# FFN up with adding DMAs: a weight sum and three low parts per pair of columns formed on GpSimd's queue

## The chip, the cores and the metric

The kernel runs on one NeuronCore of a Trainium2 chip. The core has a matrix engine (TensorE, "PE" in the profile, with its weight loads as "PEld"), a vector engine (VectorE, DVE), a scalar engine (ScalarE, ACT), a general one (GpSimd, POOL), a synchronising engine (SyncE, SP) that here only issues transfers, and 16 DMA engines that all queues share. The metric is the time of one execution on the device in microseconds (us), as the median of repeated runs. A profile of one execution shows each instruction on each engine.

## What is computed

A trunk of two decoder layers on 512 tokens of width 1024 in float32. Each layer has a mixer (dilated attention beside a state-space block in the first, a gated linear recurrence in the second) and a SwiGLU feed-forward block, each between two RMS norms. The change touches only the feed-forward block's first half:

```python
def swiglu(x, w_gate, w_up, w_down):
    return (jax.nn.silu(x @ w_gate) * (x @ w_up)) @ w_down
...
        hn = rms_norm(x, norm_ffn_pre[layer])
        ff = swiglu(hn, ffn_w_gate[layer], ffn_w_up[layer], ffn_w_down[layer])
        x = x + rms_norm(ff, norm_ffn_post[layer])
```

The hidden width is 2816, which is 22 blocks of 128 columns for the gate and 22 for the up matrix.

## The kernel before

Products are made to nearly float32 precision from a shorter format ("fp32r"): each operand is split into a high part (a rounded copy) and a low part (the operand less its high part), and three matmuls (high x high, high x low, low x high) stand for one. Activations lie transposed, features on the 128 partitions and tokens along a row of 512.

**FFN up** (`ffn_up`, line 598). The first two pairs of columns (a gate block and an up block make a pair n) are done plainly. The other 20, n = 2 to 21, go through the loop at line 694 with a fast scheme for 2x2 block matrices (Strassen's idea in Winograd's form). The blocks are a gate column's two halves over the input width, a11 and a12, an up column's two halves, a21 and a22, and the two halves of the tokens. Seven products take the place of eight. For this the weights are combined first, in `pair_weights` (line 636): s1 = a21 + a22 (line 644), s2 = s1 - a11, a21 is overwritten by a11 - a21, and s4 = a12 - s2. Each of these tiles holds 128 partitions x 512 values, as 4 blocks of 128 x 128 weights.

**Chunks.** `Raw` (line 205) takes tiles and loads them by DMAs on SP's queue, 256 KB each (line 216), 128 partitions x 4 rows of 512 bytes. `Chunk` (line 221) forms, for each raw tile, the high part on ACT (line 240) and the low part on DVE (line 241), and gives the raw tile back. A pair has four chunks. "a" is the gate column (tiles a11, a12), "c" the sums (s1, s4), "d" the up column (its first tile overwritten by a11 - a21, its second a22 as loaded), "b" has s2 alone. That makes 7 high parts on ACT and 4 + 7 operations on DVE per pair. The names in the trace carry layer, pair and chunk: `wlo_f010a` is the low part of chunk a of pair 10 in layer 0. `wraw_f` is a loaded tile, `wraw_s_f` a tile of s1 or s4, `wraw_t_f` one of s2.

**Products and what follows.** `product` (line 690) runs 4 blocks x 3 matmuls of 256 tokens; seven of them make a pair. ACT moves three of the products out of PSUM (lines 707 to 711), DVE combines the rest (lines 720 to 726), ACT takes the SiLU and DVE multiplies (lines 614 and 616).

**Order.** All engines run at once, each in the order of its own list of instructions, and wait on one another by semaphores. A scheduler makes these lists when the program is built, from a model of the times, except where the code pins an order. Tiles for raw weights and parts come from one list of places (`place`, line 194); a load waits on SP until the tile that it overwrites was last read, so prefetch runs as far ahead as there are free places. GpSimd is all but unused in this stage: it has the power of the row norm (line 383), which the first evacuations need, and in the stages before and after it some additions to the residual (line 502).

Of the kernel before, what the change touches and what calls it, by code (L numbers as in the profile page):

```python
# [11 lines left out]
F32 = mybir.dt.float32  # L12
F32R = mybir.dt.float32r
I32 = mybir.dt.int32
AF = mybir.ActivationFunctionType
ALU = mybir.AluOpType
# [3 lines left out]
P = 128  # L20
S = 512
D = 1024
NF = D // P
# [71 lines left out]
def hybrid_trunk(  # L95
# [8 lines left out]
    nc = tc.nc  # L104
    dve, act, pool = nc.vector, nc.scalar, nc.gpsimd
# [88 lines left out]
    def place(nm, dtype, base=None):  # L194
        p = next(p for p in places if base is None or p[0] is base)
        places.remove(p)
        return p[0].tile([P, S], dtype, tag=p[1], name=nm), p

    def give(ps):
        places.extend(p for p in ps if p not in retired)  # L200

    def shaped(t, n):
        return t.rearrange("p (k n) -> p k n", n=n)

    class Raw:


        def __init__(self, nk, n, nm, src=None, base=None):
            self.n, self.step = n, S // n
            self.parts, self.places = [], []  # L210
            for i in range(0, nk, self.step):
                t, p = place(f"wraw_{nm}_{i}", F32, base)
                self.parts.append(shaped(t, n))
                self.places.append(p)
                if src is not None:
                    nc.sync.dma_start(self.parts[-1], src[:, i:i + self.step])
# [4 lines left out]
    class Chunk:  # L221


        def __init__(self, raw, nm, alloc=None, view=None, base=None, eng=None):
            n, self.step = raw.n, raw.step
            eng = eng or dve
            self.places, self.parts = [], []
            for i, src in enumerate(raw.parts):
                pair = []
                for q in ("hi", "lo"):  # L230
                    if alloc is not None:
                        t = alloc(f"w{q}_{nm}_{i}")
                    else:
                        t, p = place(f"w{q}_{nm}_{i}", F32R, base)
                        self.places.append(p)
                    pair.append(shaped(t, n))
                self.parts.append(pair)
                hi, lo = pair
                if view is None:
                    act.activation(hi, src, AF.Copy)  # L240
                    eng.tensor_tensor(lo, src, hi.bitcast(F32), op=ALU.subtract)  # L241
                else:
                    for j in range(self.step):
                        r = src[:, j].rearrange("p (q g c) -> p q g c", g=8, c=CH)
                        act.activation(view(hi[:, j]), r, AF.Copy)
                        dve.tensor_tensor(view(lo[:, j]), r, view(hi[:, j]).bitcast(F32), op=ALU.subtract)
                give(raw.places[i:i + 1])
# [347 lines left out]
    def ffn_cols(layer):  # L595
        return [(w[layer], n * P) for n in range(NH) for w in (ffn_w_gate, ffn_w_up)]

    def ffn_up(layer, xh, xl, first, nsum, nm, hp):
# [4 lines left out]
        cols2 = ffn_cols(layer)  # L603
        hidden = []
        env = {}
        HK = NF // 2
# [28 lines left out]

        def pair_weights(n, alloc=None, base=None):

            r0, r1 = [Raw(NF, P, f"{nm}{n}{i}", cols2[2 * n + i][0][:, n * P:(n + 1) * P].rearrange(
                "(k p) n -> p k n", p=P), base=base) for i in range(2)]
            (a11, a12), (a21, a22) = r0.parts, r1.parts  # L640
            rs = Raw(NF, P, f"s_{nm}{n}", base=base)
            rt = Raw(HK, P, f"t_{nm}{n}")
            (s1, s4), (s2,) = rs.parts, rt.parts
            dve.tensor_tensor(s1, a21, a22, op=ALU.add)  # L644
            dve.tensor_tensor(s2, s1, a11, op=ALU.subtract)  # L645
            dve.tensor_tensor(a21, a11, a21, op=ALU.subtract)
            dve.tensor_tensor(s4, a12, s2, op=ALU.subtract)
            return [Chunk(t, f"{nm}{n}{q}", alloc=alloc) for t, q in ((r0, "a"), (rs, "c"), (r1, "d"), (rt, "b"))]

        own = iter([*range(11, NH), 3, 4, 5, 6])  # L650
        for q in range(NFIRST // 2 + 3):
            retired.add((hp, f"hh{q}"))
        wa, wc, wd, wb = pair_weights(
            NFIRST // 2, lambda name: hp.tile([P, S], F32R, tag=f"hh{next(own)}", name=name), sb)

# [3 lines left out]
        for k in range(HK):  # L659
            a = hp.tile([P, S], F32, tag=f"hh{7 + k % 2}", name=f"xa_{nm}{k}")  # L660
            b = hp.tile([P, S], F32, tag=f"hh{9 + k % 2}", name=f"xb_{nm}{k}")
            act.activation(a, xT[k], AF.Copy, scale=col("g1", layer * NF + k))
            act.activation(b, xT[k + HK], AF.Copy, scale=col("g1", layer * NF + k + HK))
            raw = Raw(4, HT, f"tr_{nm}{k}")
# [29 lines left out]
        for n in range(NFIRST // 2, NH):  # L694
            if n > NFIRST // 2:
                for q in range(n + 3):
                    retired.add((hp, f"hh{q}"))
                places[:] = [p for p in places if p not in retired]
                wa, wc, wd, wb = pair_weights(n)
# [971 lines left out]
```

## Time and profile before

| | |
|---|---|
| three runs | 1168.99, 1170.04, 1175.23 us; median 1170.04 us |
| the profiled execution | 1169.77 us in all, span from first to last instruction 1167.7 us |
| granted PE clock | 0.99 of full speed |
| DMA traffic | 113.45 MB, mean 97 GB/s; SP's queue 32.2% of the 16 engines' time |
| FFN up, layer 0 and layer 1 | about 295 to 490 us and 845 to 1040 us of the span |
| FFN weights on SP's queue | 88 loads of gate tiles, 88 of up tiles, 256 KB each, landing a median 3.1 and 3.3 us after issue |

The profile gives, for each engine, its busy time in any stretch, the instructions by source line and tile, who waited for whom, and the chain of work that ended last, followed back from the last instruction. Busy time alone does not say what a change is worth: an engine that nobody waits for can get faster without effect. A matmul's row is longer than its share of time, because matmuls overlap; the count of matmuls in a stretch says how fast PE goes on. For DMA instructions the row gives the time of issuing; when the data lands is told apart.

### The profile page before, as it was taken

What the parts mean: (1) busy time and instruction counts of PE and PEld (TensorE: products, weight loads), DVE (VectorE), ACT (ScalarE), POOL (GpSimd) and SP (SyncE); (2) the same over time, 40 slices, a digit from 0 to 9 for tenths busy, and PEclk for the clock granted to TensorE, in tenths of its full rate; (3) what the DMA queues carried; (4) which work ended last, traced back from release to release, by engine and by line L of the source; (5) the groups of instructions that cost most, each with busy time, mean ns of one, the idle gap of its engine ahead of it and who ended that gap; (6) DMA issues with size and microseconds to landing.
All of it is one profiled execution on the core that took longest, in us unless ns stands there. A gap on an engine that the chain in (4) does not pass through costs nothing.

```text
span 1167.7 us, 20255 instructions
## 1 busy us (share of the span) xinstructions
PE 1131.7 (97%) x7550; PEld 1013.2 (87%) x7550; DVE 876.8 (75%) x1841; ACT 626.6 (54%) x1290; POOL 60.6 (5%) x100
## 2 busy tenths in 40 slices
PE   6999899999999999999999999999999999999997
PEld 6877666889999999988889887889999999988886
DVE  7989675478999899882345887956999899984224
ACT  7556576357655555652244479744855455582221
POOL 1000010003000000000004000004000000000001
PEclk9999989999999999999999999999999999999999
DMA  8534410522333332423330323430253333334221
GB/s 211 144 117 134 108 45 1 172 64 63 93 109 100 101 99 83 125 92 96 121 100 1 106 86 98 126 109 1 77 146 95 101 109 91 90 119 126 91 63 72
DMA packets 165561, 113.45 MB, mean 97 GB/s; under 512 B 26852, under 2 KB 142296, under 8 KB 165464
## 3 DMA queue, kind: packets, MB, share of 16 engines
q1 hardware_dynamic: 162168, 109.95, 32.2%
q10 hardware_dynamic: 3040, 2.17, 0.7%
q8 instruction: 59, 0.97, 0.3%
q14 instruction: 38, 0.31, 0.1%
q0 software_dynamic: 256, 0.06, 0.0%
HBM read 103.75 MB, written 4.19 MB: 92 GB/s over the span
## 4 chain that ended last, share of the span: by engine, by line
PE 82%; DVE 5%; ACT 5%; DMA 4%; issue 2%; POOL 0%; ACTq 0%; DVEq 0%; POOLq 0%; SPq 0%
PE fo L170 10%; PE op_fd L170 10%; PE op_mo L170 6%; PE f00b L170 5%; PE f02b L170 5%; PE f01b L170 4%; PE f11b L170 4%; PE f10b L170 4%; PE f12b L170 4%; PE qkv L170 4%; PE gg L170 3%; PE f03b L170 2%; PE f13b L170 2%; PE mo1b L170 2%; PE mo0b L170 2%; PE xbb L170 2%
## 5 line engine op out<-in xcount | busy, mean ns | idle before, releaser
L241 DVE TENSOR_TENSOR wlo_fo<-wraw_fo,whi_fo 128x512 fp32r<-128x512 f32 x44 | 30.3, 691 | 63.8 <-PE fo L170 58.7
L170 PE MATMUL op_fd<-hi_f,whi_fd 128*128 128x512 f32 (+1 forms) x200 | 73.7, 369 | 0.0
L170 PE MATMUL op_fd<-lo_f,whi_fd 128*128 128x512 f32 (+1 forms) x200 | 73.4, 367 | 0.0
L170 PE MATMUL op_fd<-hi_f,wlo_fd 128*128 128x512 f32 (+1 forms) x200 | 73.0, 367 | 0.0
L170 PE MATMUL fo<-wlo_fo,hi_f 128*128 128x512 f32 x176 | 69.4, 394 | 0.0
L170 PE MATMUL fo<-whi_fo,lo_f 128*128 128x512 f32 x176 | 69.1, 394 | 0.0
L170 PE MATMUL fo<-whi_fo,hi_f 128*128 128x512 f32 x176 | 68.9, 396 | 0.0
L240 ACT ACTIVATE whi_fo<-wraw_fo 128x512 fp32r<-128x512 f32 x44 | 27.6, 631 | 70.6 <-DMA wraw_fo<-in_ffn_w_down_dram 43.4
L241 DVE TENSOR_TENSOR wlo_fd<-wraw_fd,whi_fd 128x512 fp32r<-128x512 f32 x44 | 30.1, 690 | 46.4 <-ACT whi_fd L240 42.5
L240 ACT ACTIVATE whi_fd<-wraw_fd 128x512 fp32r<-128x512 f32 x44 | 27.4, 629 | 54.7 <-DMA wraw_fd<-in_ffn_w_down_dram 33.8
L170 PEld LDWEIGHTS op_fd<-lo_f,whi_fd 128*128 128x128 f32 x200 | 37.7, 189 | 6.8
L170 PEld LDWEIGHTS op_fd<-hi_f,wlo_fd 128*128 128x128 f32 x200 | 37.7, 189 | 6.7
L170 PEld LDWEIGHTS op_fd<-hi_f,whi_fd 128*128 128x128 f32 x200 | 37.7, 189 | 6.6
L170 PE MATMUL qkv<-whi_qkv,xh_m 128*128 128x512 f32 x96 | 40.5, 427 | 0.0
L170 PEld LDWEIGHTS fo<-whi_fo,lo_f 128*128 128x128 f32 x176 | 33.1, 188 | 7.8
L170 PEld LDWEIGHTS fo<-whi_fo,hi_f 128*128 128x128 f32 x176 | 33.1, 188 | 7.7
L170 PEld LDWEIGHTS fo<-wlo_fo,hi_f 128*128 128x128 f32 x176 | 33.1, 188 | 7.5
L170 PE MATMUL qkv<-wlo_qkv,xh_m 128*128 128x512 f32 x96 | 38.3, 399 | 0.0
L170 PE MATMUL qkv<-whi_qkv,xl_m 128*128 128x512 f32 x96 | 38.0, 396 | 0.0
L644 DVE TENSOR_TENSOR wraw_s_f<-wraw_f,wraw_f 128x512 f32<-128x512 f32 x40 | 27.4, 684 | 11.4 <-DMA wraw_f<-in_ffn_w_up_dram 10.7
L241 DVE TENSOR_TENSOR wlo_mo<-wraw_mo,whi_mo 128x512 fp32r<-128x512 f32 x32 | 21.4, 686 | 14.5 <-ACT whi_mo L240 14.2
L645 DVE TENSOR_TENSOR wraw_t_f<-wraw_s_f,wraw_f 128x512 f32<-128x512 f32 x40 | 27.3, 682 | 6.0 <-DMA wraw_f<-in_ffn_w_gate_dram 6.0
(1974 smaller groups left out, 4297.8 us busy)
## 6 DMA issues: line engine op xcount, KB each, us to landing
wraw_f<-in_ffn_w_gate_dram SPq DMA_DIRECT2D x88, 256.0 KB, 3.1
wraw_f<-in_ffn_w_up_dram SPq DMA_DIRECT2D x88, 256.0 KB, 3.3
wraw_fd<-in_ffn_w_down_dram SPq DMA_DIRECT2D x44, 256.0 KB, 2.8
wraw_fo<-in_ffn_w_down_dram SPq DMA_DIRECT2D x44, 256.0 KB, 2.9
wraw_qkv<-in_ev_w_in_dram SPq DMA_DIRECT2D x24, 256.0 KB, 3.5
wraw_mo<-in_ev_w_out_dram SPq DMA_DIRECT2D x16, 256.0 KB, 4.3
wraw_xb<-in_od_w_in_dram SPq DMA_DIRECT2D x16, 256.0 KB, 2.8
wraw_gg<-in_od_w_in_dram SPq DMA_DIRECT2D x16, 256.0 KB, 2.8
```

The lines of the kernel that those rows point to most:

```text
L170: self.pin(nc.tensor.matmul(o, lhsT=lhsT, rhs=rhs, start=start, stop=stop, **kw))
L240: act.activation(hi, src, AF.Copy)
L241: eng.tensor_tensor(lo, src, hi.bitcast(F32), op=ALU.subtract)
L644: dve.tensor_tensor(s1, a21, a22, op=ALU.add)
L645: dve.tensor_tensor(s2, s1, a11, op=ALU.subtract)
```

## The change

Two things in the FFN up's pairs move from DVE to DMAs that add while they write, issued on GpSimd's queue.

- **The sum s1.** The tile of s1 is loaded with a21 by one more plain DMA on SP, and a22 is then added onto it from DRAM by an adding DMA on GpSimd. The addition on DVE goes.
- **Three low parts per pair**, those of tiles that are plain weights: both tiles of chunk a and the second of chunk d. ACT writes the negated high part to the low tile (a copy with scale -1 into the same short format), and an adding DMA on GpSimd adds the weights onto it from DRAM. The subtraction on DVE goes. The other four low parts (s1, s4, s2 and a11 - a21 are not in DRAM) stay on DVE.

Per pair that is four DVE operations fewer, three ACT operations more, one plain load more and four adding DMAs, of 256 KB each; 40 pairs in the two layers.

```diff
-        def __init__(self, raw, nm, alloc=None, view=None, base=None, eng=None):
+        def __init__(self, raw, nm, alloc=None, view=None, base=None, eng=None, dram=None):
...
                     act.activation(hi, src, AF.Copy)
-                    eng.tensor_tensor(lo, src, hi.bitcast(F32), op=ALU.subtract)
+                    if dram is not None and dram[i] is not None:
+                        act.activation(lo, src, AF.Copy, scale=-1.0)
+                        pool.dma_start(lo, dram[i], accum_op=ALU.add)
+                    else:
+                        eng.tensor_tensor(lo, src, hi.bitcast(F32), op=ALU.subtract)
...
         def pair_weights(n, alloc=None, base=None):
 
-            r0, r1 = [Raw(NF, P, f"{nm}{n}{i}", cols2[2 * n + i][0][:, n * P:(n + 1) * P].rearrange(
-                "(k p) n -> p k n", p=P), base=base) for i in range(2)]
+            src = [cols2[2 * n + i][0][:, n * P:(n + 1) * P].rearrange("(k p) n -> p k n", p=P) for i in range(2)]
+            rs = Raw(NF, P, f"s_{nm}{n}", base=base)
+            (s1, s4) = rs.parts
+            nc.sync.dma_start(s1, src[1][:, 0:HK])
+            pool.dma_start(s1, src[1][:, HK:NF], accum_op=ALU.add)
+            r0, r1 = [Raw(NF, P, f"{nm}{n}{i}", src[i], base=base) for i in range(2)]
             (a11, a12), (a21, a22) = r0.parts, r1.parts
-            rs = Raw(NF, P, f"s_{nm}{n}", base=base)
             rt = Raw(HK, P, f"t_{nm}{n}")
-            (s1, s4), (s2,) = rs.parts, rt.parts
-            dve.tensor_tensor(s1, a21, a22, op=ALU.add)
+            (s2,) = rt.parts
             dve.tensor_tensor(s2, s1, a11, op=ALU.subtract)
             dve.tensor_tensor(a21, a11, a21, op=ALU.subtract)
             dve.tensor_tensor(s4, a12, s2, op=ALU.subtract)
-            return [Chunk(t, f"{nm}{n}{q}", alloc=alloc) for t, q in ((r0, "a"), (rs, "c"), (r1, "d"), (rt, "b"))]
+            same = {"a": [src[0][:, 0:HK], src[0][:, HK:NF]], "d": [None, src[1][:, HK:NF]]}
+            return [Chunk(t, f"{nm}{n}{q}", alloc=alloc, dram=same.get(q))
+                    for t, q in ((r0, "a"), (rs, "c"), (r1, "d"), (rt, "b"))]
```

How the lists move is seen best on GpSimd. Around the start of layer 0's FFN up its list read, before (the residual's last additions, the row norm's power, and then already the end of the FFN):

```order
L502 TENSOR_TENSOR xT_4_151<-xT_4_151,o_mo04_2932 128x256
L502 TENSOR_TENSOR xT_5_152<-xT_5_152,o_mo05_2934 128x256
L502 TENSOR_TENSOR xT_6_153<-xT_6_153,o_mo06_2936 128x256
L502 TENSOR_TENSOR xT_7_154<-xT_7_154,o_mo07_2938 128x256
L383 TENSOR_TENSOR rsy_f0_3486<-rst_f0_3485,neghalf_133 128x4
L383 TENSOR_TENSOR rsy_fd00_7567<-rst_fd00_7566,neghalf_133 128x2
```

and now, at the same place:

```order
L506 TENSOR_TENSOR xT_7_154<-xT_7_154,o_mo07_2938 128x256
L243 DMA wlo_f02a_0_3514<-in_ffn_w_gate_dram 128x4x128
L646 DMA wraw_s_f03_0_3735<-in_ffn_w_up_dram 128x4x128
L243 DMA wlo_f02a_1_3519<-in_ffn_w_gate_dram 128x4x128
L243 DMA wlo_f02d_1_3536<-in_ffn_w_up_dram 128x4x128
L387 TENSOR_TENSOR rsy_f0_3486<-rst_f0_3485,neghalf_133 128x4
L646 DMA wraw_s_f04_0_3887<-in_ffn_w_up_dram 128x4x128
```

Four adding DMAs now stand ahead of the row norm's power. In the middle of the stage, where GpSimd's list had nothing, it now has, for pairs 8 to 12 (L243 a low part, L646 a sum):

```order
L243 DMA wlo_f08a_1_4517<-in_ffn_w_gate_dram 128x4x128
L646 DMA wraw_s_f09_0_4647<-in_ffn_w_up_dram 128x4x128
L243 DMA wlo_f08d_1_4534<-in_ffn_w_up_dram 128x4x128
L243 DMA wlo_f09a_0_4664<-in_ffn_w_gate_dram 128x4x128
L646 DMA wraw_s_f010_0_4799<-in_ffn_w_up_dram 128x4x128
L243 DMA wlo_f09a_1_4669<-in_ffn_w_gate_dram 128x4x128
L646 DMA wraw_s_f011_0_4951<-in_ffn_w_up_dram 128x4x128
L243 DMA wlo_f09d_1_4686<-in_ffn_w_up_dram 128x4x128
L243 DMA wlo_f010a_0_4816<-in_ffn_w_gate_dram 128x4x128
L243 DMA wlo_f010a_1_4821<-in_ffn_w_gate_dram 128x4x128
L646 DMA wraw_s_f012_0_5103<-in_ffn_w_up_dram 128x4x128
```

Sums of pairs 10 and 11 come ahead of low parts of pair 9, in one queue. On DVE, between the evacuations of pairs 6 and 7, the list read before (`gt`, `ut`, `pu`: tiles of the evacuation):

```order
L241 TENSOR_TENSOR wlo_f09d_1_4655<-wraw_f091_4_4625,whi_f09d_1_4654 128x512
L645 TENSOR_TENSOR wraw_t_f09_0_4629<-wraw_s_f09_0_4627,wraw_f090_0_4619 128x512
L646 TENSOR_TENSOR wraw_f091_0_4623<-wraw_f090_0_4619,wraw_f091_0_4623 128x512
L721 TENSOR_TENSOR gt_f07_4459<-f00b7_4366,bcs_f0_3495 128x256
L241 TENSOR_TENSOR wlo_f09c_0_4643<-wraw_s_f09_0_4627,whi_f09c_0_4642 128x512
L722 TENSOR_TENSOR pu_f07_4370<-pu_f07_4370,f01b7_4367 128x256
L724 TENSOR_TENSOR pu_f07_4370<-pu_f07_4370,f02b7_4368 128x256
L644 TENSOR_TENSOR wraw_s_f010_0_4775<-wraw_f0101_0_4771,wraw_f0101_4_4773 128x512
L241 TENSOR_TENSOR wlo_f010a_0_4783<-wraw_f0100_0_4767,whi_f010a_0_4782 128x512
L616 TENSOR_TENSOR hh_f06_4321<-ut_f06_4312,gt_f06_4311 128x512
```

and now, at the evacuation of pair 7:

```order
L729 TENSOR_TENSOR gt_f07_4483<-f00b7_4390,bcs_f0_3495 128x256
L245 TENSOR_TENSOR wlo_f09c_0_4674<-wraw_s_f09_0_4647,whi_f09c_0_4673 128x512
L730 TENSOR_TENSOR pu_f07_4394<-pu_f07_4394,f01b7_4391 128x256
L651 TENSOR_TENSOR wraw_t_f010_0_4811<-wraw_s_f010_0_4799,wraw_f0100_0_4803 128x512
L731 TENSOR_TENSOR ut_f07_4484<-pu_f07_4394,pv_f07_4395 128x256
L245 TENSOR_TENSOR wlo_f09c_1_4678<-wraw_s_f09_4_4648,whi_f09c_1_4677 128x512
L732 TENSOR_TENSOR pu_f07_4394<-pu_f07_4394,f02b7_4392 128x256
L653 TENSOR_TENSOR wraw_s_f010_4_4800<-wraw_f0100_4_4805,wraw_t_f010_0_4811 128x512
L245 TENSOR_TENSOR wlo_f09d_0_4682<-wraw_f091_0_4655,whi_f09d_0_4681 128x512
```

The sum of pair 10 (L644) and the low parts `wlo_f010a` and `wlo_f09d_1` are gone from DVE; the sums' consumers (L651, L653) stand at about the same distance ahead of the products.

## The prediction

> **What bounds the kernel now.** I read the page's busy times first, then the stretches of the FFN-up stages, then who waits for whom in them.
>
> ```profile
> PE 1131.7 (97%) x7550; PEld 1013.2 (87%) x7550; DVE 876.8 (75%) x1841; ACT 626.6 (54%) x1290; POOL 60.6 (5%) x100
> ```
>
> PE is busy nearly all the time. The change touches only the two FFN-up stages. The view by stretches gives, for the steady middle of each and for each as a whole, the length, then the busy time of PE, PEld, DVE, ACT and POOL, the granted clock, the DMA share and the rate in GB/s.
>
> ```profile
> 350.00:460.00 110.00, 110.00 (x927) 110.00 (x926) 102.27 (x204) 57.29 (x117) 0.00 (x0) 1.00 0.34 97
> 850.00:950.00 100.00, 99.39 (x833) 98.99 (x833) 94.73 (x189) 53.39 (x108) 0.00 (x0) 1.00 0.40 114
> 297.00:486.00 189.00, 186.16 (x1557) 185.20 (x1555) 178.66 (x353) 101.47 (x207) 0.00 (x0) 1.00 0.34 99
> 843.00:1041.00 198.00, 195.90 (x1621) 193.41 (x1620) 187.02 (x371) 110.37 (x226) 0.00 (x0) 1.00 0.38 110
> ```
>
> A pair needs 84 matmuls (7 products x 4 blocks x 3). From 350 to 460 us there are 927, so 927/84 = 11.04 pairs in 110 us: **9.97 us of PE per pair**. PE has no gap there. DVE comes close, 102.27/11.04 = 9.26 us per pair, ACT uses 5.19 us, POOL nothing, and the DMA engines a third. So the stage is PE-bound, with DVE a hair behind. All that PE idles in the two stages is 189 - 186.16 = 2.8 us and 198 - 195.90 = 2.1 us. By PEld it is 3.8 and 4.6 us. **The most that a lighter DVE can bring is thus 5 to 8 us**, and not all of that is DVE's. The gaps lie at the stage's start and end, and the chain that ended last shows what they are (start, length, what):
>
> ```profile
> 291.86 0.89 PE bc_f L170 x8
> ...
> 307.82 3.64 DMA wraw_f<-in_ffn_w_gate_dram
> ...
> 312.70 0.28 ACT pu_f L709
> ...
> 467.35 2.80 DMA wraw_f<-in_ffn_w_up_dram
> ```
>
> Both large ones begin with a load of a raw weight tile, and only then pass ACT and DVE.
>
> **What is taken off DVE and put on ACT.** Rows of the raw weight tiles between 350 and 400 us (durations in ns, minimum, median, maximum):
>
> ```profile
> L644 DVE TENSOR_TENSOR wraw_s_f<-wraw_f,wraw_f x5: 679/681/682, 351.3 to 391.6; 128x512 f32<-128x512 f32 x5
> L240 ACT ACTIVATE whi_f010a<-wraw_f x2: 632/633/634, 353.0 to 357.4; 128x512 fp32r<-128x512 f32 x2
> L241 DVE TENSOR_TENSOR wlo_f010a<-wraw_f,whi_f010a x2: 678/678/679, 359.2 to 363.6; 128x512 fp32r<-128x512 f32 x2
> DMA to landing us min/median/max: 2.8/3.1/4.5
> ```
>
> Per pair DVE loses the sum (L644) and three low parts (two of a, the second of d): 4 x 0.68 = 2.7 us, so 9.26 becomes 6.5 us. ACT gains three negated copies of the form of L240: 3 x 0.63 = 1.9 us, so 5.19 becomes 7.1 us. Both stay under PE's 9.97 us, so I count ACT's addition at nothing. Its cover is the 2.9 us per pair that ACT still has idle; only at the stage's start, where ACT already ends a wait of PE, could it cost a negation's 0.63 us or two. What DVE gains has no row that waits for it in the middle.
>
> **What is put on the DMA engines** is the term that decides. From 350 to 460 us they were busy 0.34 x 110 = 37.4 us and moved 97 GB/s x 110 us = 10.67 MB, or 40.7 loads of 256 KB: **0.92 us of all 16 engines per load**. The stretch from 850 us gives the same (40 us for 43.5 loads). Four loads per pair are 3.7 us of 9.97. The change adds one plain load, so 5 x 0.92 = 4.6 us, and four adding DMAs of the same shape, 128 partitions x 4 rows of 512 bytes. No adding DMA is in the trace. From below one costs as much as a load, 0.92 us, since it fetches the same rows. From above, adds that do not overlap each other take the landing time of a load each, 3.1 us. I take **twice a load, 1.84 us**, nearer to the lower row: where a load reads one operand and writes one, an add reads two, the DRAM row and the tile, and writes one. The pair then needs 4.6 + 4 x 1.84 = **11.96 us of DMA engines**, 2.0 us more than PE. The pace passes from PE to the DMA engines; DVE's relief is then worth nothing. The engines can be kept that full, as the first microseconds show:
>
> ```profile
> 6.00:10.00 4.00, 2.40 (x11) 1.94 (x11) 3.29 (x18) 2.15 (x5) 0.00 (x0) 1.00 0.91 282
> 10.00:14.00 4.00, 4.00 (x30) 4.00 (x29) 3.92 (x13) 4.00 (x13) 0.00 (x0) 1.00 0.91 302
> ```
>
> Of 40 pairs the first of each stage is prepared ahead of it, so 38 x 1.99 = **+76 us**. An add at 1.33 us is the break-even, (9.97 - 4.6)/4. At the upper end, 3.1 us an add, the pair needs 17.0 us and the sum is +267 us; at 1.5 us an add, +24 us.
>
> The Trainium skill, in Collectives: The Full Stack, section "The bandwidth ceiling: the fold count and why AG ≠ RS ≠ AR", says that an add in the DMA engines is slow for its two source reads, not for the adding, with 62.28 GB/s for a copying collective against 32.35 for an adding one. By that ratio of 1.93 a pair would need 11.7 us and the sum would be +66 us; no run here shows an add yet.
>
> **What is put on POOL's queue.** POOL's only DMAs so far are eight small ones at the start, issued back to back:
>
> ```profile
> L303 POOL DMA_DIRECT2D vec<-in_rg_conv_w_dram x1: 509/509/509, 3.0 to 3.0; - x1
> L303 POOL DMA_DIRECT2D vec<-in_rg_conv_b_dram x1: 527/527/527, 3.5 to 3.5; - x1
> L303 POOL DMA_DIRECT2D vec<-in_rg_b_r_dram x1: 499/499/499, 4.0 to 4.0; - x1
> L383 POOL TENSOR_TENSOR rsy_f<-rst_f,neghalf x2: 1058/1234/1409, 286.0 to 822.2; 128x4 f32<-128x4 f32 x2
> ```
>
> One of 32 rows of 512 bytes takes POOL 0.51 us, and one of 8 rows 0.50 to 0.53: no growth with rows is seen. An add has 512 rows. If the cost stays flat, four are 2.0 us of POOL per pair, hidden; if it grew in proportion, 512/32 x 0.51 = 8.2 us each, 33 us per pair, +860 us in all. POOL becomes the pace above 9.97/4 = 2.49 us per add. I take it as hidden, by the flat rows, and keep the rest for a rival. The power of the row norm (L383), queued behind four adds now, starts at 286.0 us, and what it leads to on PE (bc_f) comes at 291.86 us: about 4 us of cover for four issues at 0.51 us, so nothing; without cover, 2 us in each layer.
>
> **The wait that is added.** A low part was written by DVE right behind its high part; now it waits in POOL's one queue, behind sums of later pairs. How long a finished low part lay before PE took it:
>
> ```profile
> L170 PE MATMUL f00b<-xh_mo,wlo_f010a x8: 278/281/285, 374.8 to 381.7; 128*128 128x256 f32 x8
> L170 PE MATMUL f00b<-xh_mo,wlo_f015a x8: 279/283/285, 425.9 to 431.6; 128*128 128x256 f32 x8
> L241 DVE TENSOR_TENSOR wlo_f015a<-wraw_f,whi_f015a x2: 674/674/675, 418.0 to 419.6; 128x512 fp32r<-128x512 f32 x2
> ```
>
> Pair 10's was done at 364.3 us and used from 374.8 on, pair 15's done at 420.3 and used at 425.9: 10.5 and 5.6 us of lead. A negation (0.63), an issue (0.51) and a landing like a load's (3.1) make 4.2 us in place of DVE's 0.68: 3.6 us of the lead go, and it suffices while the engines have room. I cost it at nothing for that reason.
>
> **The rivals.** (1) **Adds as cheap as loads; not slower.** Below 1.33 us an add, the DMA engines stay under 9.97 us (8.3 us at 0.92), every transfer is hidden, and DVE's 2.7 us per pair come free. The gaps of PE bound the gain: about half of the 5 us by PE's rows, as the two large gaps begin with a load. It ends at 1167 us, between 1162 and 1174. For it speaks the third of DMA time used now; against it the second read. (2) **POOL's issue is the pace.** 512 rows per add, against at most 32 in any row of the trace. At 4 us an add a pair takes 16 us, 38 x 6.0 = +229 us, about 1399 us. For it speaks that the rows per add grow 16-fold past anything seen; against it the flat 0.50 to 0.53 us. (3) **The queue blocks its head.** An add for a later pair's sum waits for its first half, whose load waits until PE has freed a tile:
>
> ```profile
> SPq L216 <- PE f11b L170: 42.8, 11, 16.4
> ```
>
> SP waits up to 16.4 us for such a tile, and the low parts behind the sum wait with it. From the point at which such a block outlasts the lead of 5.6 us, PE stands still. If every second pair loses 1.2 us, the sum is 19 x 1.2 = +23 us, about 1193 us. Without a shortage of DMA time the order on POOL has sums only one to three pairs ahead, which speaks against more.
>
> **How the numbers follow.** The profiled execution took 1169.8 us (span 1167.7), the median of the three runs is 1170.0: one number. The likeliest case, adds at twice a load, gives 1169.8 + 76 = **1246 us**, with 0.47; its own range is 1190 (1.5 us an add) to 1316 (2.3 us an add, 13.8 us a pair). Rival 1 has 0.20, rival 2 has 0.22, rival 3 has 0.11. The range from 1167 to 1400 us leaves out half of rival 1 below and half of rival 2 above, about 0.2. A measurement of this kernel tells 0.5%, 5.9 us, from no change. Slower by more: all of rival 2, nearly all of the forecast and of rival 3, 0.76. Within: most of rival 1 and a little of the others, 0.18. Faster by more needs over 5.9 us, more than the gaps by PE's own rows, so 0.06.
>
> **What would show it.** Right: in the steady stretches of the new profile the DMA share is above 0.9, PE's matmuls per 100 us fall from some 840 to about 700, PE waits for low parts or for ACT and DVE behind late sums, DVE's busy time falls by over a quarter, and adds land later than 3.1 us. Rival 1 shows a DMA share of 0.8 or less and PE without gaps; rival 2 shows POOL's DMA instructions back to back at over 2.5 us with the DMA engines half idle; rival 3 shows neither full, with single gaps of PE behind a sum. The forecast is wrong if an add costs the engines less than 1.33 us or POOL more than 2.5 us.

## The result, and the profile after

The changed kernel takes a median of 1283.5 us (four runs, 1272.6 to 1291.9) against 1171.8 us for the kernel before on the same chip: a ratio of **1.092, 95% interval 1.083 to 1.101**, and a loss of 108 us. The run of 1291.9 us, and one run of the kernel with the low parts alone further down, fell in a slower state of the chip: the medians count them, ratios and losses do not. The forecast was 1246 us, with a range from 1167 to 1400. The profiled execution took 1279.5 us, its span 1277.7.

The page of the changed kernel, first the busy times, then PE, DVE, the granted clock and the DMA engines in 40 slices of the span, then the DMA queues (packets, MB, share of the 16 engines' time):

```profile
PE 1170.9 (92%) x7550; PEld 1046.4 (82%) x7550; DVE 791.8 (62%) x1681; ACT 688.9 (54%) x1410; POOL 267.7 (21%) x260
...
PE   7999899998879898899999999997987898889997
...
DVE  7999565567556556582346878746746575565223
...
PEclk9999899998989899999999999988988999899999
DMA  8535203509999999933320333517899999883321
...
q1 hardware_dynamic: 183288, 120.43, 33.2%
q0 software_dynamic: 84736, 42.01, 26.6%
```

PE's row has its dips where the DMA row stands at 8 or 9: the two FFN-up stages. DVE has grown light there, and it did not help. The last row is the new one: GpSimd's queue, which had moved 0.06 MB, now moves 42 MB and takes 26.6% of the 16 engines' time. The same two stages by stretches (columns as above):

```profile
350.00:460.00 110.00, 94.77 (x721) 92.90 (x721) 66.49 (x134) 59.75 (x121) 44.02 (x34) 0.92 1.01 176
...
300.00:540.00 240.00, 206.33 (x1571) 202.45 (x1572) 146.55 (x295) 137.21 (x279) 94.51 (x73) 0.92 1.02 182
900.00:1130.00 230.00, 195.42 (x1518) 191.12 (x1518) 133.86 (x269) 122.30 (x248) 90.53 (x70) 0.95 1.01 179
```

From 350 to 460 us PE gets through 721 matmuls instead of 927, DVE is busy 66.5 us instead of 102.3, and the DMA engines are full, 1.01 instead of 0.34. Transfers land later, too (median us from issue to landing):

```profile
wraw_f<-in_ffn_w_gate_dram SPq DMA_DIRECT2D x88, 256.0 KB, 4.5
wraw_f<-in_ffn_w_up_dram SPq DMA_DIRECT2D x88, 256.0 KB, 5.0
...
wraw_s_f<-in_ffn_w_up_dram POOLq DMA_DIRECT2D x40, 256.0 KB, 6.8
```

PE seldom waits for an add by name: four of its waits, 7.0 us in all, name an adding DMA, while 28 waits of 55.0 us in all name ACT's moves of products out of PSUM. What stands behind such a move is shown by the timeline of the changed kernel at 374 us (start, length, what, and in brackets the idle time before it with its end; rows of SP, PE and PEld between them left out):

```profile
373.79 0.69 DVE L651 TENSOR_TENSOR wraw_t_f<-wraw_s_f,wraw_f 128x512 f32<-128x512 f32 x1 [0.55 <-DMA wraw_s_f<-in_ffn_w_up_dram]
...
374.73 0.69 DVE L245 TENSOR_TENSOR wlo_f08b<-wraw_t_f,whi_f08b 128x512 fp32r<-128x512 f32 x1
375.45 0.63 ACT L240 ACTIVATE whi_f010a<-wraw_f 128x512 fp32r<-128x512 f32 x1 [2.95 <-DVE wlo_f08b L245]
375.99 0.36 ACT L717 ACTIVATE pu_f<-f01b 128x256 f32<-128x256 f32 x1
...
376.40 0.39 PE L170 MATMUL f01b<-th_f,whi_f07d 128*128 128x256 f32 x1 [2.70 <-ACT pu_f L717]
```

A late sum holds DVE (0.55 us here), DVE holds a high part on ACT that waits for a tile (2.95 us), and behind that, in ACT's order, stands the move of a finished product out of PSUM. PE needs that bank: 2.7 us of standstill, booked to ACT, begun by a DMA.

### The profile page after: what moved, and what is told of

Read it like the earlier page. It is cut to its first block, busy times and chain, and to the rows that moved or that the text cites. A ratio compares the mean times of both kernels' runs of the same rounds, so it can differ in the third digit from the quotient of the medians.

```text
span 1277.7 us, 20721 instructions
## 1 busy us (share of the span) xinstructions
PE 1170.9 (92%) x7550; PEld 1046.4 (82%) x7550; DVE 791.8 (62%) x1681; ACT 688.9 (54%) x1410; POOL 267.7 (21%) x260
## 3 DMA queue, kind: packets, MB, share of 16 engines
q1 hardware_dynamic: 183288, 120.43, 33.2%
q0 software_dynamic: 84736, 42.01, 26.6%
## 5 line engine op out<-in xcount | busy, mean ns | idle before, releaser
L646 POOL DMA_DIRECT2D wraw_s_f<-in_ffn_w_up_dram x40 | 59.0, 1474 | 313.4 <-DMA wraw_s_f<-in_ffn_w_up_dram 149.3
L651 DVE TENSOR_TENSOR wraw_t_f<-wraw_s_f,wraw_f 128x512 f32<-128x512 f32 x40 | 27.5, 688 | 83.1 <-DMA wraw_s_f<-in_ffn_w_up_dram 76.8
L652 DVE TENSOR_TENSOR wraw_f<-wraw_f,wraw_f 128x512 f32<-128x512 f32 x40 | 27.6, 690 | 67.5 <-DMA wraw_f<-in_ffn_w_up_dram 51.6
L618 ACT ACTIVATE gt_f<-gt_f 128x512 f32<-128x512 f32 x44 | 27.0, 622 | 23.1 <-DVE gt_f L733 23.0
```

The costliest lines, as they stand in the source:

```text
L618: act.activation(gt, gt, AF.Silu)
L646: pool.dma_start(s1, src[1][:, HK:NF], accum_op=ALU.add)
```

## The experiments

Two theories stood against each other. **Engine time**: the adds take more of the 16 DMA engines than a pair's 9.97 us of PE can hide. 26.6% of 1277.7 us over 160 adds is 2.12 us each, so a pair needs 5 x 0.92 + 4 x 2.12 = 13.1 us. **Queue or latency**: what costs is the wait, since an add starts only after a load or a negation and lands late, and others stand behind it in their order. In what follows, "demand" is the DMA engines' time per pair worked out in this way; each verdict compares with runs of the kernel before on the same chip.

**Copies in place of adds.**

```diff
-                        pool.dma_start(lo, dram[i], accum_op=ALU.add)
+                        pool.dma_start(lo, dram[i])
...
-            pool.dma_start(s1, src[1][:, HK:NF], accum_op=ALU.add)
+            pool.dma_start(s1, src[1][:, HK:NF])
```

> The four adding DMAs of each pair become plain copies of the same rows on the same queue, with the same waits and the same order (so s1 and three low parts hold wrong values: the first half of the sum and the negated high parts are overwritten). Theory 'engine time': in the changed kernel an add costs 26.6% of 1277.7 us / 160 = 2.12 us of all 16 DMA engines, a load 0.92, so a pair needs 4.6 + 8.5 = 13.1 us against 9.97 us of PE. With copies it needs 9 x 0.92 = 8.3 us: the DMA share in the stage falls below 0.9, PE is the pace again, 1165 to 1185 us. Rival 'queue': what costs is the order and the waits on POOL's one queue (sums that wait for their load stand ahead of low parts) and its 1.3 to 2.5 us per issue; those stay, so the time stays above 1250 us.

Measured: 1206.7 us, ratio 1.033 (1.029 to 1.036). Same queue, order and waits, and two thirds of the loss are gone; but it misses both figures. A copy's own cost explains part of that. Its queues:

```profile
q1 hardware_dynamic: 183288, 120.43, 34.9%
q0 software_dynamic: 66816, 42.01, 19.2%
```

19.2% of 1208.2 us is 232 us for 160 copies, not 0.92 but 1.45 us each on average. Demand was about 10.4 us, still over PE's. Why, a later run shows.

**Only the sum, or only the low parts.** The sum alone:

```diff
-            same = {"a": [src[0][:, 0:HK], src[0][:, HK:NF]], "d": [None, src[1][:, HK:NF]]}
+            same = {}
```

> Only the sum s1 is formed by an adding DMA (one plain load and one add more per pair); all low parts stay on DVE. Engine time: 5 x 0.92 + 2.12 = 6.7 us per pair, under PE's 9.97: 1165 to 1176 us. Queue: DVE's 76.8 us of waiting for sums in the changed kernel comes from the sum's own chain (load, then add), which stays: 1200 us or more.

The three low parts alone, with the sum on DVE as before:

```diff
-            nc.sync.dma_start(s1, src[1][:, 0:HK])
-            pool.dma_start(s1, src[1][:, HK:NF], accum_op=ALU.add)
...
+            dve.tensor_tensor(s1, a21, a22, op=ALU.add)
```

> Only the three low parts are formed by adding DMAs; the sum is on DVE again. Engine time: 4 x 0.92 + 3 x 2.12 = 10.0 us per pair, just PE's 9.97: 1170 to 1195 us, DMA share in the stage 0.9 to 1.0. Queue: without sums ahead of low parts in POOL's list the block is gone: 1165 to 1175 us with the DMA share just as high.

Measured: the sum alone 1196.7 us, 1.024 (1.021 to 1.027); the low parts alone 1208.6 us, 1.033 (1.030 to 1.037). Neither run came out as either theory had it. **Engine time by itself failed here**: the sum's demand is 6.7 us, and from 350 to 450 us the sum-only kernel ran with the DMA engines at 0.62 and PE at its full pace:

```profile
350.00:450.00 100.00, 99.52 (x837) 99.31 (x836) 91.56 (x185) 55.16 (x110) 11.60 (x9) 1.00 0.62 142
```

Its 28 us must be lost elsewhere. The chain that ended last, in the second layer's stage (start, length, what), shows one such place whole:

```profile
891.30 0.95 PE f13b L170 x8
892.26 3.04 DMA wraw_s_f<-in_ffn_w_up_dram
...
895.36 0.49 issue
895.85 5.92 DMA wraw_s_f<-in_ffn_w_up_dram
...
901.80 0.03 ACT whi_f18c L240
...
902.33 0.37 ACT pu_f L715
...
902.75 2.17 PE f10b L170 x12
```

The first half is loaded, 3.0 us; then the add is issued and lands, 5.9 us; then ACT takes the high part of the sum and, behind it, the move that PE waits for. From the load's start to the add's landing that is 9.5 us, **the latency of a load and an add in a row**, where DVE had needed 0.68 us. Most of it was hidden: PE had products of pairs 6 and 7 until 900.8 us and then stood still for 1.95 us, as its own row says:

```profile
902.75 0.39 PE L170 MATMUL f10b<-xh_mo,whi_f16a 128*128 128x256 f32 x1 [1.95 <-ACT pu_f L715]
```

The adds' price is the same in both kernels: the software queue's 7.2% of 1194.6 us over 40 is 2.15 us, and 21.2% of 1208.3 us over 120 is 2.13 us.

**One load less, all adds kept.** The first half of the sum is copied by ACT from the loaded tile.

```diff
-            nc.sync.dma_start(s1, src[1][:, 0:HK])
+            act.activation(s1, a21, AF.Copy)
```

> As the changed kernel, with all four adds per pair, but the first half of the sum comes from the loaded tile by a copy on ACT in place of the extra plain load: one load of 256 KB less per pair. Engine time: 12.2 in place of 13.1 us per pair, 38 x 0.92 to 1.2 = 35 to 45 us less than the changed kernel: 1238 to 1250 us. Queue: the same number of adds in the same queue, the sum's add now waits for a load and for ACT: no gain, 1280 us or more.

Measured: 1255.8 us, 1.075 (1.071 to 1.079): a loss of 87 us instead of the changed kernel's 108. Both ranges were missed. The sign is that of engine time, in a kernel whose chain of waits had become longer by a step on ACT; the 21 us saved are some six tenths of 35 us. The loss as a whole fits engine time better: 4 x 0.92 + 4 x 2.13 is 12.2 us, and 38 x (12.2 - 9.97) = 85.

**Fewer low parts, and the sum without its add.**

```diff
-            same = {"a": [src[0][:, 0:HK], src[0][:, HK:NF]], "d": [None, src[1][:, HK:NF]]}
+            same = {"a": [src[0][:, 0:HK], src[0][:, HK:NF]]}
```

> Two low parts per pair (chunk a) by adding DMAs; sum and all else on DVE. With an add at 2.13 us of the DMA engines, as the run with three low parts showed, a pair needs 3.7 + 4.3 = 8.0 us, under PE's 9.97. Theory 'engine time alone': the loss is gone, 1165 to 1178 us. Theory 'engine time and latency' (an add lands 5 to 7 us after its issue and the list of ACT or DVE stands behind it, which the start of a stage, with nothing prepared ahead, cannot hide): 1178 to 1195 us, with the loss at the first pairs of each stage and 10.0 us per pair after them.

and `same = {"a": [src[0][:, 0:HK], None]}` for one:

> One low part per pair (the first tile of chunk a) by an adding DMA. 3.7 + 2.13 = 5.8 us of DMA engines per pair. Engine time alone: 1164 to 1174 us, at best 5 us under the kernel before. Engine time and latency: 1172 to 1185 us.

The extra load kept, the addition on DVE (and `same = {}`, so that no adding DMA is left):

```diff
-            pool.dma_start(s1, src[1][:, HK:NF], accum_op=ALU.add)
...
+            dve.tensor_tensor(s1, s1, a22, op=ALU.add)
```

> The sum's tile is loaded with a21 by the extra plain load on SP, as in the changed kernel, but a22 is added on DVE; no adding DMA at all. Theory 'latency of load, then add': the add was what made the sum-only kernel 27 us slower, so this one is back at 1165 to 1176 us. Rival 'places and order': the sum's tile is taken from its load on and the loads on SP stand in another order, with less prefetch; that stays, 1185 to 1200 us.

The sum's add as a plain copy (`pool.dma_start(s1, src[1][:, HK:NF])`), all else as in the sum-only kernel:

> As the sum-only kernel, but the adding DMA becomes a plain copy on the same queue with the same waits (s1 is a22 alone, the addition left out). What the copy costs the DMA engines is read from the software queue's share: 0.9 to 1.0 us if the second read makes an add dear, about 2.1 us if the software queue does. Time: with latency as the cause, the copy lands some 3 us earlier than an add and 1175 to 1190 us come out; with places and order as the cause 1190 to 1200 us as before.

Measured: two low parts 1184.3 us, 1.014 (1.010 to 1.019); one 1181.3 us, 1.012 (1.007 to 1.017); extra load with DVE's add 1172.5 us, 1.004 (1.002 to 1.007); the sum as a copy 1180.4 us, 1.011 (1.006 to 1.016). So of the sum's 28 us some 5 belong to the extra load, the earlier taken tile and the other order, and the rest to the add. A copy on the same queue lands after a median 4.0 us where the add took 5.5, and costs 13 us instead of 28. Where the low parts lose is seen in the times at which PE comes to the end of each pair (start of the pair's last matmul, us of the span, layer 0):

| pair | before | two low parts | one low part | changed kernel |
|---|---|---|---|---|
| 4 | 328.7 | 341.4 | 335.5 | 334.5 |
| 8 | 365.7 | 379.4 | 372.4 | 394.7 |
| 11 | 398.7 | 409.9 | 402.5 | 434.1 |
| 16 | 447.4 | 459.9 | 452.3 | 488.7 |
| 20 | 488.9 | 499.7 | 492.1 | 542.9 |

With two low parts or one the whole delay, 12.7 or 6.8 us, is there by pair 4. None is added after it, and from pair 8 on a pair takes 10.0 us, PE's own pace. At the start PE's waits name adds directly: the longest, for the low part of pair 5's chunk a, is 4.0 us with two low parts and 2.4 us with one. In the changed kernel the delay goes on growing: from pair 4 to 20 it takes 208.4 us for 16 pairs, 13.0 each, which is the demand of 13.1. The sum-only kernel, read in the same way, is 3.7 us behind at pair 4 of layer 0 and 3.9 at pair 20; in layer 1 it is 21.9 and 25.6 us behind, so it too loses its time up to the first pairs of a stage.

The copies' queues in the run with the sum as a copy also give the price that was asked for:

```profile
q1 hardware_dynamic: 183288, 120.43, 35.0%
q0 software_dynamic: 3456, 10.55, 3.0%
```

3.0% of 1176.4 us over 40 is **0.88 us per copy**, as a load on SP; an add of the same bytes on the same queue cost 2.15. The queue alone is not what makes it dear. The copies of the first run cost 1.45 us on average because 120 of them also turned float32 into the shorter format: (232 - 40 x 0.88)/120 = 1.64 us each, an estimate that takes the other 40 at the 0.88 us of this run.

**Adds that nobody reads; and adds only once the stage is under way.** The kernel before, with the changed kernel's extra load, negations and adds onto five tiles of their own (room for them was made by 6 instead of 10 places):

```diff
                     eng.tensor_tensor(lo, src, hi.bitcast(F32), op=ALU.subtract)
+                    if dram is not None and dram[i] is not None:
+                        u = shaped(spare_tile[0](f"u_{nm}_{i}", F32R), n)
+                        act.activation(u, src, AF.Copy, scale=-1.0)
+                        pool.dma_start(u, dram[i], accum_op=ALU.add)
...
+            us = shaped(spare_tile[0](f"us_{nm}{n}", F32), P)
+            nc.sync.dma_start(us, src[1][:, 0:HK])
+            pool.dma_start(us, src[1][:, HK:NF], accum_op=ALU.add)
```

> The kernel before with all its DVE work, and beside it, per pair, the changed kernel's extra load, its four adding DMAs and its three negations, onto five tiles of their own that nothing reads. To make room for them the list of places has 6 instead of 10 tiles of the stage's own. No product, sum or low part waits for an add. Engine time: 5 x 0.90 + 4 x 2.14 = 13.1 us of DMA engines per pair still sets the pace, some 90 to 120 us above the kernel with 6 places and no adds. Latency alone: nothing waits for an add's data, so within 15 us of that kernel.

Its base, with `EXTRA = 6` alone:

> The kernel before with 6 instead of 10 of the stage's own places, nothing else: the base for the run with unread adds. All theories: less prefetch, 1168 to 1185 us.

Two low parts, with `if n >= 9 else {}` behind the table `same`:

> Two low parts per pair by adding DMAs, as in the kernel that was 16 us slower, but only from pair 9 on in each layer; 8.0 us of DMA engines per pair. If that kernel lost its time in the first pairs, to the add's latency while nothing is prepared ahead, this one is at 1165 to 1174 us. If an add costs something wherever it stands, 1176 us or more.

The whole change from pair 9 on, the sum on DVE below that:

> All of the change, but only from pair 9 on in each layer; pairs 2 to 8 as before. Engine time: 13 pairs in each layer need 13.1 us, less some two pairs prepared ahead: 2 x 11 x 3.1 = 68 us, 1225 to 1250 us. If the changed kernel lost its time to latency at the start of the stages, 1170 to 1190 us.

Measured: unread adds **1277.7 us**, 1.093 (1.089 to 1.097), against 1173.0 us for their base: +105 us although nothing computed depends on an add. From 300 to 540 us:

```profile
300.00:540.00 240.00, 204.08 (x1539) 199.97 (x1538) 178.14 (x349) 126.89 (x260) 93.53 (x72) 0.91 1.00 176
```

DMA engines full and PE as slow as in the changed kernel, with all of DVE's work still there: 1539 matmuls are 18.3 pairs, 13.1 us each, just the demand. One wait for adds is left in this kernel: the five tiles are used in turn, so extra loads on SP, and a few negations on ACT, waited until an earlier add had landed (some 80 us of waits on SP in all, 27.1 of them for sums), and at the start of layer 0, from 301 to 337 us, the chain that ended last runs through such adds. From 338 us on it runs through loads that land late, 7 to 10 us the longest, and the DMA share is 0.99. With the last run below, whose adds have no tiles of their own, that settles the main part as engine time. Two low parts from pair 9 on: 1167.0 us, 1.000 (0.997 to 1.003), the cost of the same adds in all pairs gone. That settles where the small part is lost: at the stage's start. That it is the add's latency rests on this, on PE's waits for adds there, and on the plain copy that landed sooner and cost less. In the stretch where the adds run (350 to 460 us) that kernel has

```profile
350.00:460.00 110.00, 109.56 (x922) 109.36 (x921) 94.22 (x191) 68.17 (x137) 26.98 (x21) 1.00 0.75 147
```

three quarters of the DMA engines in use, DVE lighter by 8 us, and PE no faster. The whole change from pair 9 on: 1227.9 us, 1.051 (1.046 to 1.055), +60 us where engine time said 68 and latency at the start at most 20; from 360 to 520 us its DMA engines were at 1.00, and a pair took 12.7 us (1061 matmuls). The share adds up the packets' times and passes 1 for short whiles (1.34 from 320 to 340 us of the changed kernel); that full engines bound the pace is shown by these times per pair, beside the share.

## Why the prediction was right, and where not

- **The bound and the ceiling: right.** PE sets the stage's pace, and a lighter DVE brings nothing: the kernel with two low parts from pair 9 on had one with all transfers hidden and gained nothing. No kernel tried beat the one before; the 5 to 8 us of gaps, which begin with loads, were not touched.
- **DMA engine time as the term that decides: right, and its size was off.** The step that was mis-sized is the price of an add, taken as twice a load, 1.84 us. It is 2.12 to 2.15 us in every kernel with adds. With it the sum is 38 x (13.1 - 9.97) = +119 us, against 108 measured; with 1.84 it was +76. The reason given for the price, the second read, is not shown: a copy that only changes the format cost 1.64 us with one read, and the low parts' adds, which change the format too, cost no more than the sum's, which do not (2.13 and 2.15). By the ratio of 1.93 the Trainium skill (Collectives: The Full Stack, "The bandwidth ceiling: the fold count and why AG ≠ RS ≠ AR") had given +66 us. The direction agrees, but in rows of 512 bytes the ratio to a copy is 2.15/0.88 = 2.4.
- **ACT's three negations at nothing: right as work** (59.8 us busy of 110). But ACT's order is what carried a late sum to PE.
- **POOL's issue hidden: right, on a wrong price.** An add takes POOL 1.28 us or more, not 0.51, and a copy of the same rows 0.75; 44 of 110 us is still no bound. The rival that had POOL as the pace falls. So does the one of the blocked queue as the main cause, by its own sign: it had neither POOL nor the DMA engines full.
- **The added wait at nothing: wrong.** The lead of 5.6 to 10.5 us was read off pairs 10 and 15. At the start of a stage it does not suffice: 13 us lost with one low part, 28 with the sum, while the DMA engines had room. With the engines full this does not come on top as far as is seen: the unread adds, whose data nobody waits for, cost 105 us, as much as the changed kernel.
- **The row norm's power behind four adds at nothing: doubtful.** The matmuls that use it (bc_f) came at 295.2 instead of 291.7 us, and ACT's copy of their result at 303.9 instead of 294.6. Whether that cost time of its own was not tried. With one low part bc_f came on time, at 291.6 us, and the pairs were late all the same.
- **The signs to look for**: the DMA share of 0.9 and more, late landings, DVE lighter by over a quarter (35%), waits behind late sums: all there. But over half of DVE's 35% is only that fewer pairs were done: per pair it fell from 9.26 to 7.75 us (66.49 us over 721/84 = 8.58 pairs), 16%, and not to 6.5. PE did 655 matmuls per 100 us, not 700.

What remains open is the copies' kernel: its demand of 10.4 us explains 38 x 0.4 = 15 of its 38 us, and the start's latency would be the rest; that was not tried by itself.

## What to carry to other kernels

An adding DMA is no free adder: price it in time of the 16 DMA engines, here 2.1 us per 256 KB in rows of 512 bytes against 0.9 for a load, add up the stage's demand, and compare it with the time of the engine that sets the pace. Moving work from a nearly full engine to the DMA engines helps only if somebody waits for that engine; if nobody does, the best outcome is no change. And read the lead of a new wait at the start of a stage, where nothing is prepared ahead, not in its middle.

## What the runs showed of the hardware that was not expected

- A DMA that turns float32 into the shorter format costs the engines 1.64 us per 256 KB where a plain copy on the same queue costs 0.88. The plain copies went as 80 packets each ((3456 - 256)/40), the adds as 528 ((84736 - 256)/160), and so did the copies that change the format ((66816 - 256 - 40 x 80)/120). The number of packets alone is not the price: SP's extra loads count 528 each too ((183288 - 162168)/40), at 0.9 us.
- The granted PE clock fell in the stages where PE waited, from 1.00 to 0.92 (300 to 540 us of the changed kernel) and 0.91 with the unread adds. A short wait is enough for it, without traffic: after the stand of 1.95 us shown above, the clock in the sum-only kernel was 0.50 from 904 to 907 us, while the DMA engines idled at first (columns as before):

```profile
904.00:905.00 1.00, 1.00 (x7) 1.00 (x6) 1.00 (x4) 1.00 (x4) 0.00 (x0) 0.50 0.00 0
```

  So a wait can cost more than its own length. An estimate from the mean clocks, 0.983 against 0.990 before, is (0.017 x 1194.6) - (0.010 x 1167.7) = 9 of the sum-only kernel's 28 us. In the changed kernel, at 0.959, it comes to 41 us, in stages that the DMA engines paced anyway.
- With the DMA engines full, the sum's add landed a median 6.8 us after its issue, and 5.5 us with them at 0.62.
